# A two-block decoder kernel: the inverses of 32-token blocks built row by row, or row by row within 16 tokens and joined by products

## The chip, the cores and the metric

The kernel runs on one core of a Trainium2 chip. The metric is the device time of one execution in microseconds. The engines named below are TensorE (PE, with PEld for its weight loads), VectorE (DVE), ScalarE (ACT), GpSimd (POOL) and SyncE (SP), which only issues transfers here.

## The reference, cut to what matters

The reference is a decoder of several blocks over 16 meta tokens and 256 tokens of width 1024: feed-forward blocks, one RWKV-7 time mixing, sparse attention, and a second block with two kinds of attention. Only the time mixing is touched. Its core is a recurrence by token over a 64x64 state for each of 16 heads:

```python
def step(S, inp):
    r_t, w_t, k_t, v_t, a_t, b_t = inp
    sa = jnp.einsum("bhij,bhj->bhi", S, a_t)
    S = S * w_t[:, :, None, :] + sa[..., None] * b_t[:, :, None, :] + v_t[..., None] * k_t[:, :, None, :]
    y = jnp.einsum("bhij,bhj->bhi", S, r_t)
    return S, y
```

with `a = -kk` (the normalised removal keys) and `b = kk * a`. All is float32.

## The kernel before, in words

The kernel does not step token by token. It takes the 16 meta tokens as one chunk and the 256 others as four chunks of 64. Within a chunk the removals depend on each other through a strictly lower triangular matrix (the products of b with a), so each chunk and head needs the inverse of a unit lower triangular 64x64 matrix. `aab(m)` makes these products for the heads 2m and 2m+1, in blocks of 32 tokens: the 128 diagonal blocks (16 heads, 4 chunks, 2 blocks) go to `Dg`, those beside them to `Tt`. `inverses` inverts the diagonal blocks, and `doubles` makes the 64-token inverses of them by products (`da`, `db`).

`inverses` works with one block on each of the 128 partitions. `start` transposes `Dg` by 32x32 squares to `af` and sets `tf` to unit matrices. `rows` then runs over the rows s of a block: all rows below s get `a[:, s, i]` times row s added, as one multiplication into `u` (L868) and one addition (L871), each in two halves; for the last five rows one combined operation for every row below (L885). `end` transposes the result back twice, into `D1` (L891) and `Dt` (L892), and copies `Dt` into the diagonal blocks of `Tt`, half by ScalarE (L899), half by GpSimd (L901). `meta` does the same for the blocks of 16 of the meta chunk, on tiles named `am`.

The code is a list of steps in the order of the table `ORDER`: `solve0` to `solve8` are the steps that `inverses` returns, set among units of weights such as `v7` or `r0` (a unit: load 512 KB of weights, split them into two parts `wh` and `wl`, at L173 or L175 and L182, and multiply, at L261 to L263), the gates' low-rank products `g1a` and `g1b` (L614), evacuations such as `evr0`, and the steps of the recurrence (`ck`, `cv`, `cw`, `cr`, `cs`, `ct`, `cy`, `cn`). A scheduler of the framework then orders all instructions by a simulated timeline; each engine executes its own list strictly in that order. The tiles `mm` are PSUM banks (eight in rotation), `wl` has three buffers and `wh` four.

Names in the rows: `xmh`, `xml` are the two parts of the values' input, `xh`, `xl` those of the receptances'; `Tm` is the inverse of the meta chunk and `room` work space of the recurrence; `s`, `t` and `u` are temporary tiles.

Of the kernel before, what the change touches and what calls it, by code (L numbers as in the profile page):

```python
# [10 lines left out]
F32 = mybir.dt.float32  # L11
F32R = mybir.dt.float32r
I32 = mybir.dt.int32
AF = mybir.ActivationFunctionType
ALU = mybir.AluOpType
# [87 lines left out]
class Unit:  # L103
    """Weights to stream in, the products with them, and what follows some units later; held: units before that
    this one's products still read."""
# [6 lines left out]
class Core:  # L112
    def __init__(self, ctx, tc, io):
# [25 lines left out]
        self.eps = self.const.tile([128, 2], F32, name="eps")  # L139
# [8 lines left out]
    def call(self, fn, ahead=0):  # L148
        """fn between units; before it the parts of as many of those that follow, if they are not there yet."""
        self.items.append((fn, ahead))  # L150
# [16 lines left out]
    def hi(self, u):  # L167
        """Weights in two parts that single-pass products carry exactly: the first."""
        if not u.lo:
            return  # L170
        u.wh = self.wring.tile([128, 1024], F32R, tag="wh", name="wh", bufs=WH)[:u.p, :u.n]
        if u.hi == "A":
            self.A.activation(u.wh, u.wf[:u.p, :u.n], AF.Copy)  # L173
        else:
            self.V.tensor_copy(u.wh, u.wf[:u.p, :u.n])  # L175

    def lo(self, u):
        """And the second."""
# [5 lines left out]
    def run(self):  # L184
        units = [x for x in self.items if isinstance(x, Unit)]
        n = len(units)
# [3 lines left out]
        def ahead(i, most=WH):  # L190
            """Loads, first and second parts as far ahead of unit i as their rings reach."""
# [44 lines left out]
    def evac(self, name, out, x, scale=None):  # L236
        """Copies x, by ScalarE or VectorE."""
# [17 lines left out]
    def one(self, pool, name, shape, dt=F32):  # L255
        """A tile that keeps its place as long as the pool."""
# [12 lines left out]
    def accum(self, out, wh, wl, xh, xl, kn, n, k0=0, total=None):  # L269
        """out[m] += sum over k of w[k][m] x[k], weights standing, up to n columns of x moving."""  # L270
# [6 lines left out]
    def rsqrt(self, out, x, scale, eps):  # L277
        """1 / sqrt(x * scale + eps), with a Newton step."""
# [24 lines left out]
    def rms(self, n):  # L303
        """1 / rms by token, on every partition."""
# [5 lines left out]
    def split_tile(self, k, gain, t0, n):  # L310
        """Tile k of h * gain in two parts; its squares added up."""
# [11 lines left out]

    def swiglu(self, win, wout, t0, n, hook, first=()):
        """Reads the split of h that the step before left; hook(k) follows each finished tile of h."""
# [50 lines left out]
    def out_units(self, w, kn, src, scale, t0, n, hook, k0=0, eng=lambda m: {}):  # L376
        """h += scale * x @ w, x split and by features, w given as [m][128][kn][128]; a step a tile of h."""
# [28 lines left out]
    def play(self, order, steps, units):  # L406
        """Emits the steps by name: those of units as they come, the others as calls between them."""
# [7 lines left out]

    def rwkv(self, gain, hook):
# [21 lines left out]
        # the mixed inputs of the projections  # L438
# [6 lines left out]
        def mixes(i, kind, e=None):  # L445
            """Mixed input i, a tile a call: whole, or in two parts."""
# [35 lines left out]
        def first_mix():  # L482
            """The normalised input; the mixed inputs of the keys, the decays and the removals."""
            hn, xx, last = R["hn"], R["xx"], []
            hi, lo = R["x", 2] = [self.xs.tile([128, KT, T], F32R, tag=n, name=n) for n in ("xh", "xl")]
            def mix(x, i, k):
                """Mixed input i, by VectorE, or by ScalarE and GpSimdE."""
# [69 lines left out]
        # keys  # L557
# [18 lines left out]
        def first(n, parts):  # L576
            """The first tiles of the keys and the low-rank pairs of two inputs side by side, as the inputs come."""
# [23 lines left out]
        # low-rank pairs, in float32 products  # L601
        def l1_unit(c0, parts, k0, k1, last, after=()):
            """Columns c0.. of the first factors: parts are (bank, row, width, input)."""
# [67 lines left out]
        # a, b, k by decays within a chunk  # L671
# [5 lines left out]
        def units(q):  # L677
            """1 / norm of the keys."""
# [22 lines left out]
        def over(e, j, x, s):  # L701
            """KB[place j] = x / decay, for the pairs s; the factor -1/2 of place 0 comes with the products."""
# [19 lines left out]
        # strictly lower parts of b a by chunk: diagonal blocks of 32 tokens apart from those beside them  # L722
# [43 lines left out]
        # values, receptance, bonus  # L766
# [24 lines left out]
        # gates  # L791
# [63 lines left out]
    def inverses(self, R):  # L855
        """Inverses of unit lower triangular blocks of 32 tokens (16 in the meta chunk), one per partition."""
        V, G = self.V, self.G
# [18 lines left out]

        def rows(s0, s1):
            a, t = R["af"], R["tf"]
            for s in range(s0, s1):
                if s < B - 5:  # L880
                    u = self.tmp("u")[:, :(B - 1 - s) * (s + 1)].rearrange("p (a b) -> p a b", b=s + 1)
                    row(V, a, t, u, s + 1, s, (s + 1, (s + B + 1) // 2, B))
                else:
                    for i in range(s + 1, B):
                        V.scalar_tensor_tensor(t[:, i, :s + 1], t[:, s, :s + 1], a[:, s, i:i + 1], t[:, i, :s + 1],  # L885
                                               op0=ALU.mult, op1=ALU.add)

        def end():
            D1, Dt = R["D1"], R["Dt"] = R["Dg"], R["af"]
            tf, Tt = R["tf"], R["Tt"]  # L890
            V.transpose(D1, tf.rearrange("p s t -> p t s"))  # L891
            V.transpose(Dt, tf)  # L892
            Dt = Dt.rearrange("p t (m c) -> p m c t", c=NC)
# [26 lines left out]
        cuts = (0, 5, 10, 15, 20, 25, 31)  # L920
        return [start, meta] + [lambda a=a, b=b: rows(a, b) for a, b in zip(cuts[:-1], cuts[1:])] + [end]

    def chunks(self, R):
        """The recurrence over chunks of 64 tokens after the 16 of the meta tokens.
# [1121 lines left out]
```

## Time and profile before

| | |
|---|---|
| three runs | 1602.51, 1602.21, 1589.57 us; median 1602.21 |
| span of the profiled execution | 1588.7 us (30959 instructions), mean granted TensorE clock 0.971 |
| TensorE products busy | 1527.4 us (96%) |
| VectorE busy | 1020.3 us (64%) |
| ScalarE busy | 732.4 us (46%) |
| GpSimd busy | 334.0 us (21%) |

The profile is of one execution; its span is to be compared with the lowest of the three runs. A busy TensorE is one with a product in flight, not one at its peak. A float32 product leaves two records in the trace. The granted clock is 1.00 at 2.4 GHz and 0.50 at 1.2 GHz. Times in the views are counted from the start of the span.

### The profile page before, as it was taken

What the parts mean: (1) busy time and instruction counts of PE and PEld (TensorE: products, weight loads), DVE (VectorE), ACT (ScalarE), POOL (GpSimd) and SP (SyncE); (2) the same over time, 40 slices, a digit from 0 to 9 for tenths busy, and PEclk for the clock granted to TensorE, in tenths of its full rate; (3) what the DMA queues carried; (4) which work ended last, traced back from release to release, by engine and by line L of the source; (5) the groups of instructions that cost most, each with busy time, mean ns of one, the idle gap of its engine ahead of it and who ended that gap; (6) DMA issues with size and microseconds to landing.
All of it is one profiled execution on the core that took longest, in us unless ns stands there. A gap on an engine that the chain in (4) does not pass through costs nothing.

```text
span 1588.7 us, 30959 instructions
## 1 busy us (share of the span) xinstructions
PE 1527.4 (96%) x12612; PEld 1427.2 (90%) x12612; DVE 1020.3 (64%) x1857; ACT 732.4 (46%) x1266; POOL 334.0 (21%) x346
## 2 busy tenths in 40 slices
PE   7999989699999999999999999899999999999999
PEld 7999967568788999999999987579999978899999
DVE  6655478997444655556555569667665489886643
ACT  6544428333223544445444434655445335566532
POOL 2111034752011111001111043142110334320000
PEclk9999989798888999999999999999999999999999
DMA  7645534121101445555545552036556552265552
GB/s 224 216 173 166 178 96 141 63 92 69 41 1 41 173 173 175 171 175 191 175 174 165 172 166 77 21 112 234 186 183 180 175 167 91 85 215 186 187 195 101
DMA packets 70851, 230.63 MB, mean 145 GB/s; under 512 B 7827, under 2 KB 12468, under 8 KB 70580
## 3 DMA queue, kind: packets, MB, share of 16 engines
q1 hardware_dynamic: 68480, 225.35, 42.7%
q10 hardware_dynamic: 2228, 3.29, 0.9%
q8 instruction: 99, 1.62, 0.4%
q14 instruction: 44, 0.36, 0.1%
HBM read 226.52 MB, written 2.10 MB: 144 GB/s over the span
## 4 chain that ended last, share of the span: by engine, by line
PE 82%; DVE 12%; ACT 2%; DMA 2%; issue 1%; POOL 1%; SPq 0%; DVEq 0%; POOLq 0%; ACTq 0%
PE mm L261 22%; PE mm L262 22%; PE mm L263 22%; DVE wl L182 1%; PE mm L1064 1%; PE mm L1892 1%; PE mm L1063 1%; PE mm L1166 1%; PE mm L1165 1%; PE mm L1167 1%; DVE tf L871 1%; DMA wf<-ffn_in 1%; PE mm L994 1%; DVE u L868 1%; PE mm L1869 1%
## 5 line engine op out<-in xcount | busy, mean ns | idle before, releaser
L173 ACT ACTIVATE wh<-wf 128x1024 fp32r<-128x1024 f32 (+2 forms) x404 | 411.8, 1020 | 538.3 <-issue 284.3
L261 PE MATMUL mm<-xh,wh 128*128 128x272 f32 (+2 forms) x1888 | 544.4, 290 | 14.7 <-ACT wh L173 9.0
L182 DVE TENSOR_TENSOR wl<-wf,wh 128x1024 fp32r<-128x1024 f32 (+2 forms) x388 | 463.1, 1194 | 140.7 <-PE mm L263 96.5
L262 PE MATMUL mm<-xl,wh 128*128 128x272 f32 (+2 forms) x1888 | 542.0, 288 | 3.1 <-DVE xl L440 2.7
L263 PE MATMUL mm<-xh,wl 128*128 128x272 f32 (+2 forms) x1888 | 542.4, 288 | 1.7 <-DVE wl L182 1.7
L261 PEld LDWEIGHTS mm<-xh,wh 128*128 128x128 f32 (+1 forms) x1888 | 356.8, 190 | 21.9 <-ACT wh L173 9.9
L262 PEld LDWEIGHTS mm<-xl,wh 128*128 128x128 f32 (+1 forms) x1888 | 357.2, 189 | 7.5 <-DVE xl L440 3.8
L263 PEld LDWEIGHTS mm<-xh,wl 128*128 128x128 f32 (+1 forms) x1888 | 357.5, 190 | 3.2 <-DVE wl L182 2.7
L261 PE MATMUL mm<-hh,wh 128*128 128x272 f32 (+1 forms) x704 | 201.9, 287 | 0.0
L263 PE MATMUL mm<-hh,wl 128*128 128x272 f32 (+1 forms) x704 | 201.7, 287 | 0.0
L262 PE MATMUL mm<-hl,wh 128*128 128x272 f32 (+1 forms) x704 | 201.7, 287 | 0.0
L352 POOL TENSOR_TENSOR s<-s,rstd 128x272 f32<-128x272 f32 (+1 forms) x88 | 74.6, 849 | 442.8 <-ACT s L351 442.8
L182 POOL TENSOR_TENSOR wl<-wf,wh 128x1024 fp32r<-128x1024 f32 (+3 forms) x58 | 121.3, 2093 | 146.5 <-PE mm L263 63.5
L261 PEld LDWEIGHTS mm<-hh,wh 128*128 128x128 f32 x704 | 132.6, 188 | 0.0
L263 PEld LDWEIGHTS mm<-hh,wl 128*128 128x128 f32 x704 | 132.5, 188 | 0.0
L262 PEld LDWEIGHTS mm<-hl,wh 128*128 128x128 f32 x704 | 132.5, 188 | 0.0
L360 DVE TENSOR_TENSOR u<-mm,s 128x272 f32<-128x272 f32 (+1 forms) x88 | 38.5, 437 | 123.8 <-PE mm L263 108.2
L298 POOL TENSOR_TENSOR acc<-acc,sq 128x272 f32<-128x272 f32 (+1 forms) x48 | 41.4, 863 | 262.9 <-ACT sq L296 247.1
L350 DVE TENSOR_TENSOR t<-mm,rstd 128x272 f32<-128x272 f32 (+1 forms) x88 | 38.2, 436 | 69.8 <-PE mm L263 69.7
L261 PE MATMUL mm<-hid,wh 128*128 128x256 f32 x256 | 72.0, 281 | 0.0
L262 PE MATMUL mm<-hid,wh 128*128 128x256 f32 x256 | 72.0, 281 | 0.0
L263 PE MATMUL mm<-hid,wl 128*128 128x256 f32 x256 | 72.0, 281 | 0.0
(482 smaller groups left out, 2320.4 us busy)
## 6 DMA issues: line engine op xcount, KB each, us to landing
wf<-ffn_in SPq DMA_DIRECT2D x176, 512.0 KB, 3.6
wf<-ffn_out SPq DMA_DIRECT2D x64, 512.0 KB, 3.5
wf<-b_ff SPq DMA_DIRECT2D x64, 512.0 KB, 4.7
wf<-ffn_out SPq DMA_DIRECT2D x32, 384.0 KB, 3.1
wf<-rk_k SPq DMA_DIRECT2D x8, 512.0 KB, 3.4
wf<-rk_v SPq DMA_DIRECT2D x8, 512.0 KB, 3.8
wf<-rk_r SPq DMA_DIRECT2D x8, 512.0 KB, 3.2
wf<-rk_o SPq DMA_DIRECT2D x8, 512.0 KB, 3.2
```

The lines of the kernel that those rows point to most:

```text
L173: self.A.activation(u.wh, u.wf[:u.p, :u.n], AF.Copy)
L182: (self.V if u.lo == "V" else self.G).tensor_tensor(u.wl, u.wf[:u.p, :u.n], u.wh.bitcast(F32), op=ALU.subtract)
L261: self.mm(out, wh, xh, start=start, stop=False)
L262: self.mm(out, wh, xl, start=False, stop=False)
L263: self.mm(out, wl, xh, start=False, stop=stop)
L298: self.G.tensor_tensor(self.acc[:, :n], self.acc[:, :n], self.sq[:, :n], op=ALU.add)
L350: V.tensor_tensor(t[:, :n], st.pop(("g", m))[:, :n], r, op=ALU.mult)
L352: G.tensor_tensor(s[:, :n], s[:, :n], r, op=ALU.mult)
L360: V.tensor_tensor(u[:, :n], st.pop(("u", m))[:, :n], st.pop(("s", m))[:, :n], op=ALU.mult)
L868: e.tensor_tensor(tmp[:, x - o:y - o, :w], a[:, s, x:y, None].to_broadcast([P, y - x, w]), t[:, s:w, :w].to_broadcast([P, y - x, w]), op=A ...
L871: e.tensor_tensor(t[:, x:y, :w], t[:, x:y, :w], tmp[:, x - o:y - o, :w], op=ALU.add)
L994: mm(ps[h][:, j * w:(j + 1) * w], flat(src(c, m)[OWN[h]]), R["AR"][OWN[h], m, j0:j0 + n, tok(c)], start=True, stop=True)
```

## The change

Rows are done only within blocks of 16 tokens. Both halves of a 32-token block are handled by one operation (an access pattern with a step of 16 rows and 16 columns), so `rows` runs over 15 rows with one multiplication and one addition each. The part below, between the two halves, is then made by products on TensorE: `turned` transposes and multiplies the part of `Dg` below by the first inverse (L906), `joined` copies that to `tf`, clears the other half of `tf`, and multiplies by the second inverse, once for `Dt` in all four groups of 32 partitions (L916) and once in the other orientation for `Dg` in two groups (L918), and `added` adds the results (L924, L927). `end` keeps only the copies to `Tt`. A third column of `eps` holds a mask made of `tri` (L877). The number of steps stays nine, so `ORDER` is unchanged. The rest of the diff drops comments.

```diff
-        self.eps = self.const.tile([128, 2], F32, name="eps")
+        self.eps = self.const.tile([128, 3], F32, name="eps")
...
             begin(G, R["tf"], B)
 
+            G.tensor_scalar(self.eps[:, 2:3], self.tri[:, 0, n:n + 1], -1.0, 1.0, op0=ALU.mult, op1=ALU.add)
+
         def rows(s0, s1):
+
             a, t = R["af"], R["tf"]
+
+            def both(x, i, j, *dims):
+
+                at = x[:, i:i + 1, j:j + 1]
+                return bass.AP(tensor=at.tensor, offset=at.offset, ap=[at.ap[0], [n * B + n, 2]] + [list(d) for d in dims])
+
             for s in range(s0, s1):
-                if s < B - 5:
-                    u = self.tmp("u")[:, :(B - 1 - s) * (s + 1)].rearrange("p (a b) -> p a b", b=s + 1)
-                    row(V, a, t, u, s + 1, s, (s + 1, (s + B + 1) // 2, B))
-                else:
-                    for i in range(s + 1, B):
-                        V.scalar_tensor_tensor(t[:, i, :s + 1], t[:, s, :s + 1], a[:, s, i:i + 1], t[:, i, :s + 1],
-                                               op0=ALU.mult, op1=ALU.add)
+                m, w = n - 1 - s, s + 1
+                u = self.tmp("u")[:, :2 * m * w].rearrange("p (b i j) -> p b i j", b=2, j=w)
+                below = both(t, w, 0, (B, m), (1, w))
+                V.tensor_tensor(u, both(a, s, w, (1, m), (0, w)), both(t, s, 0, (0, m), (1, w)), op=ALU.mult)
+                V.tensor_tensor(below, below, u, op=ALU.add)
+
+        quads = [slice(32 * q, 32 * q + 32) for q in range(4)]
+        byblk = lambda p: p.rearrange("p (c j) -> p c j", j=n)
+
+        def turned():
+
+            tf, Dg, Dt = R["tf"], R["Dg"], R["af"]
+            V.transpose(Dg[:, :n], tf[:, :, :n].rearrange("p s t -> p t s"))
+            V.transpose(Dt, tf)
+            p = R["p16"] = self.psum()
+            for c in range(32):
+                for r in quads:
+                    mm(p[r, c * n:c * n + n], Dg[r, :, c], Dg[r, :n, c], start=True, stop=True)
+
+        def joined():
+            tf, Dg, Dt = R["tf"], R["Dg"], R["af"]
+            V.transpose(Dg[:, n:], tf[:, :, n:].rearrange("p s t -> p t s"))
+            self.A.activation(tf[:, :, :n], byblk(R.pop("p16")), AF.Copy)
+            G.memset(tf[:, :, n:], 0.0)
+            p, o = R["p16"] = self.psum(), self.psum()
+            for c in range(32):
+                for r in quads:
+                    mm(p[r, c * n:c * n + n], tf[r, c], Dt[r, n:, c], start=True, stop=True)
+                for r in quads[::2]:
+                    mm(o[r, c * n:c * n + n], Dt[r, :, c], tf[r, c, :n], start=True, stop=True)
+
+        def added():
+            Dg, Dt = R["Dg"], R["af"]
+            p, o = R.pop("p16")
+            x = Dt[:, n:].rearrange("p t c -> p c t")
+            V.tensor_tensor(x, byblk(p), x, op=ALU.add)
+            for r in quads[::2]:
+                x = Dg[r, :n].rearrange("p t c -> p c t")
+                V.scalar_tensor_tensor(x, byblk(o)[r], self.eps[r, 2:3], x, op0=ALU.mult, op1=ALU.add)
 
         def end():
-            D1, Dt = R["D1"], R["Dt"] = R["Dg"], R["af"]
-            tf, Tt = R["tf"], R["Tt"]
-            V.transpose(D1, tf.rearrange("p s t -> p t s"))
-            V.transpose(Dt, tf)
-            Dt = Dt.rearrange("p t (m c) -> p m c t", c=NC)
+            R["D1"], R["Dt"] = R["Dg"], R["af"]
+            Tt = R["Tt"]
+            Dt = R["Dt"].rearrange("p t (m c) -> p m c t", c=NC)
...
-        cuts = (0, 5, 10, 15, 20, 25, 31)
-        return [start, meta] + [lambda a=a, b=b: rows(a, b) for a, b in zip(cuts[:-1], cuts[1:])] + [end]
+        cuts = (0, 5, 10, 15)
+        return [start, meta] + [lambda a=a, b=b: rows(a, b) for a, b in zip(cuts[:-1], cuts[1:])] + [turned, joined, added, end]
```

The lists of the engines change as follows. TensorE, at the end of the gates' low-rank products (L614), before:

```order
L614 MATMUL mm<-xm,wf 32x272
L614 MATMUL mm<-xm,wf 64x272 x2
L614 MATMUL mm<-xm,wf 32x272
L261 MATMUL mm<-xmh,wh 128x272
L262 MATMUL mm<-xml,wh 128x272
```

The unit v7 (L261 and L262 with `xmh` and `xml`) came directly behind them. And now:

```order
L614 MATMUL mm<-xm,wf 32x272
L906 MATMUL mm<-tf 32x16 x128
L916 MATMUL mm<-af,tf 32x16 x4
L918 MATMUL mm<-tf,af 32x16 x2
L916 MATMUL mm<-af,tf 32x16 x4
L918 MATMUL mm<-tf,af 32x16 x2
```

All 320 new products (the four and two of L916 and L918 come 32 times) stand ahead of v7, r0 and the recurrence's first products, which keep their order among themselves.

VectorE, from the eighth row of the meta chunk (`am`) on, before:

```order
L868 TENSOR_TENSOR am<-am 128x8x8
L868 TENSOR_TENSOR u<-af,tf 128x84
L868 TENSOR_TENSOR u<-af,tf 128x91
L871 TENSOR_TENSOR am<-am 128x8x8
L871 TENSOR_TENSOR tf<-tf,u 128x12x7
L871 TENSOR_TENSOR tf<-tf,u 128x13x7
```

and now, from a row later:

```order
L892 TENSOR_TENSOR u<-af,tf 128x128
L871 TENSOR_TENSOR am<-am 128x7x9
L893 TENSOR_TENSOR tf<-tf,u 128x2x8x8
L868 TENSOR_TENSOR am<-am 128x6x10
L892 TENSOR_TENSOR u<-af,tf 128x126
L871 TENSOR_TENSOR am<-am 128x6x10
```

Each operation on the blocks is now one in place of two, and the rows of the blocks end with those of the meta chunk in place of 16 rows later.

GpSimd, behind the clearing of the keys' tile `KBt`, before:

```order
L963 MEMSET KBt 128x1024
L182 TENSOR_TENSOR wl<-wf,wh 128x1024
L1003 MEMSET room 128x512
L182 TENSOR_TENSOR wl<-wf,wh 128x1024 x2
L977 MEMSET UV 64x1024
L182 TENSOR_TENSOR wl<-wf,wh 128x1024 x2
L901 COPY Tt<-af 32x16x32 x4
```

and now:

```order
L957 COPY Tm<-s 128x8x8
L1002 MEMSET KBt 128x1024
L912 MEMSET tf 128x32x16
L940 COPY Tt<-af 32x16x32 x4
L1042 MEMSET room 128x512
L182 TENSOR_TENSOR wl<-wf,wh 128x1024 x3
```

The four copies to `Tt` (L901 before, L940 now) stood behind five second parts `wl` of weights and now stand ahead of them, as ScalarE's four copies (L899, now L938) do ahead of the first part of r3's weights.

## Rows read from the trace of the kernel before

**Rows 1.** The page's chain that ended last: shares of the span by engine.
```profile
PE 82%; DVE 12%; ACT 2%; DMA 2%; issue 1%; POOL 1%; SPq 0%; DVEq 0%; POOLq 0%; ACTq 0%
```

**Rows 2.** The chain from 300 to 400 us: shares by line.
```profile
by line: DVE tf L871 15.3%; DVE u L868 12.1%; PE mm L261 6.7%; PE mm L262 6.1%; PE mm L263 5.8%; POOL s L916 4.1%; DVE kbx L706 4.0%; DVE AR L717 3.5%; PE mm L1126 3.3%; PE mm L1037 2.6%; ACT Tt L899 2.4%; DVE tf L743 2.3%; PE mm L994 2.1%;
```

**Rows 3.** TensorE by stretch: length, busy us (records), granted clock, DMA share, GB/s.
```profile
314.67:320.00 5.33, 5.33 (x25) 0.54 0.02 5
332.55:371.84 39.29, 32.35 (x325) 0.87 0.20 68
344.00:348.00 4.00, 4.00 (x28) 0.64 0.29 116
360.00:368.00 8.00, 7.24 (x53) 0.57 0.20 68
378.00:382.00 4.00, 4.00 (x22) 0.62 0.40 131
```

**Rows 4.** Timeline of TensorE: start, us, instruction, [idle before <-releaser].
```profile
343.68 0.60 PE L262 MATMUL mm<-xl,wh 128*128 128x272 f32 x1 [2.74 <-DVE xl L440]
360.76 2.60 PE L1037 MATMUL mm<-room,Tm 16*16 16x64 f32 x32 [3.65 <-DVE room L241]
```

**Rows 5.** VectorE's groups by line from 319 to 367 us: busy, mean ns.
```profile
L871 DVE TENSOR_TENSOR tf<-tf,u 128x110 f32<-128x110 f32 (+32 forms) x54 | 19.7, 399 | 0.1
L868 DVE TENSOR_TENSOR u<-af,tf 128x110 f32<-128x110 f32 (+32 forms) x54 | 15.7, 329 | 0.0
```

**Rows 6.** Timeline of VectorE in the rows of the inverses.
```profile
319.62 0.18 DVE L868 TENSOR_TENSOR am<-am 128x15 f32<-128x15 f32 x1
320.06 0.19 DVE L868 TENSOR_TENSOR am<-am 128x28 f32<-128x28 f32 x1
320.17 2.48 DVE L868 TENSOR_TENSOR u<-af,tf 128x15 f32<-128x15 f32 x2
322.67 0.26 DVE L871 TENSOR_TENSOR tf<-tf,u 128x15 f32<-128x15 f32 x2
339.62 0.48 DVE L868 TENSOR_TENSOR u<-af,tf 128x128 f32<-128x128 f32 x2
340.03 2.65 DVE L871 TENSOR_TENSOR tf<-tf,u 128x128 f32<-128x128 f32 x2
366.46 2.04 DVE L891 STREAM_TRANSPOSE tf<-tf 128x1024 f32<-128x1024 f32 x1
```

**Rows 7.** Timeline of GpSimd in the same stretch.
```profile
320.22 2.39 POOL L182 TENSOR_TENSOR wl<-wf,wh 128x1024 fp32r<-128x1024 f32 x1 [4.67 <-PE mm L263]
337.20 1.10 POOL L916 COPY s<-am 128x128 f32<-128x128 f32 x1 [4.62 <-DVE am L871]
371.47 4.88 POOL L901 COPY Tt<-af 32x512 f32<-32x512 f32 x4
```

**Rows 8.** Timeline of TensorE: small products, each with what starts behind it.
```profile
306.78 0.35 PE L738 MATMUL mm<-AR,kbx 64*32 64x32 f32 x7
306.99 0.35 PE L738 MATMUL mm<-AR,kbx 64*32 64x32 f32 x7
...
348.11 0.69 PE L1008 MATMUL mm<-AR,kbx 64*16 64x16 f32 x64
348.73 0.39 PE L261 MATMUL mm<-xh,wh 128*128 128x272 f32 x1
...
372.45 1.07 PE L1118 MATMUL mm<-tf,Tt 32*32 32x32 f32 x32
373.46 0.69 PE L1048 MATMUL mm<-UV,KBt 128*64 128x64 f32 x16
```

**Rows 9.** Timeline of ScalarE: an eviction of a whole PSUM bank.
```profile
458.55 0.60 ACT L239 ACTIVATE room<-mm 128x512 f32<-128x512 f32 x1 [0.55 <-PE mm L1020]
```

**Rows 10.** The tile `tri`: time to landing; and GpSimd's timeline at the start.
```profile
DMA to landing us min/median/max: 7.1/7.1/7.1
9.59 1.70 POOL L298 TENSOR_TENSOR acc<-acc,sq 128x272 f32<-128x272 f32 x2 [3.08 <-ACT sq L296]
```

More of the change, by code (lines that the diff above doesn't have):

```diff
@@ L855, in inverses @@
     def inverses(self, R):
-        V, G = self.V, self.G
+        V, G, mm = self.V, self.G, self.mm
         NC, B, n = SEQ // 64, 32, NMETA
```

## The prediction

> **What bounds the kernel now.** I read the page's shares first, then the chain that ended last, then the stretch it points to. Over the whole span TensorE carries 82% of the chain and VectorE 12% [rows 1], so a saving on VectorE counts only where the chain runs through VectorE. The chain from 300 to 400 us shows that stretch: the two lines of the row-by-row inverses, L871 and L868, are its largest shares, 15.3% and 12.1% of 100 us, and the copies of the finished inverses on ScalarE (L899) stand in it too [rows 2]. What the chain does not say is how much TensorE would do there if VectorE were never late. From the end of the gates' low-rank products (332.55) to the first product with the keys by token (371.84) there are 39.29 us, of which TensorE is busy 32.35 [rows 3]. The 6.9 us of idle are almost all in two waits for VectorE, 2.74 and 3.65 [rows 4]. Part of the busy time is slow time: the granted clock is 0.64 on the mean from 344 to 348 and 0.57 from 360 to 368, so part of it at 1.2 GHz; at full clock the work of these two windows, 4.00 and 7.24 us, would take 1.4 and 3.1 less [rows 3]. So TensorE has 32.35 - 4.5 = 27.8 us of work in these 39.3, and **11.5 us is the most that any relief of VectorE can win here**. The 35 us that VectorE is busy with L868 and L871 for the blocks [rows 5] would be the wrong figure to take.
>
> **The change, part by part.**
>
> Removed from VectorE: 108 operations of L868 and L871 and the ten of L885. Not all of their time is work: a pair on 15 and 16 elements took 2.48 us while GpSimd ran a `wl` of 2.39 from the same moment; the next such pair took 0.26 [rows 6, 7]. GpSimd's `wl` stay, so stalls of 2.2 us stay too.
>
> Added on VectorE, the rows: 30 operations, interleaved with 30 of the meta chunk as before. Three small ones that depend on each other start 0.44 us apart, first to third (319.62 to 320.06); a pair of 128 elements takes 0.41 from start to start (339.62 to 340.03) [rows 6]. A step is now two operations of the meta chunk and two of the blocks, so 0.44 at the ends and some 0.66 in the middle; I take 0.57, and 15 steps give 8.6 us from 319.6. To that come a stall behind the `wl` at 320.22 (2.2), a second behind the next `wl` (2.2), and the meta chunk's two small transposes, which now stand among the rows together with the copies that they wait for, 1.10 us each by the undisturbed row [rows 7]: some 2.3. Rows done: 319.6 + 8.6 + 2.2 + 2.2 + 2.3 = 334.9, where L891 followed them at 366.46 before.
>
> Added on VectorE, the rest: a transpose of half the blocks, half of the 2.04 us of L891 [rows 6], ends at 335.9. The full transpose, four small operations for r0 and the gates, and the second half transpose follow by some 340. After the products come L924 and two L927. They end long before anything needs them.
>
> Moved on TensorE: 320 small products now stand between the low-rank products and v7 (L906, 128 of them; then L916 and L918, 192), and TensorE takes its instructions in order. That gives four terms.
> - Wait for the first half transpose: 335.9 - 332.55 = **3.3 us**. Queued behind it are v7, r0 and everything of the recurrence. Without the second stall and the waits for the copies it would be nothing; with them longer, 4.
> - L906, 256 records (a float32 product leaves two). No row has 32 x 32 tiles in four places with 16 columns. The nearest below is L1008, 16 weights and 16 columns over four tiles: 64 records, then the next product 0.62 us after the first, 9.7 ns each. The nearest above is L1118, 32 weights and 32 columns over two tiles, one operand strided as here: 32 records in 1.01 us, 31.6 ns. Between them lies L738 with L741, 32 weights over four tiles: 12 records from 306.78 to 306.99, 17.5 ns, at the half clock that stood there [rows 8]. I take the last, whose weights and tiles are most alike: **4.5 us** (2.5 to 8.1).
> - Wait until those are copied and the other half is cleared: ScalarE's copy of 128x512 takes 0.60 [rows 9], with the handing over **0.8 us** (0.3 to 1.5). The clearing on GpSimd, behind the second half transpose at some 340, lies beside L906 and this copy.
> - L916 and L918, 384 records at the same price: **6.7 us** (3.7 to 12.1).
>
> What the products do to the clock: behind the small products that end at 314, full-width products ran from 314.67 to 320 at a mean of 0.54, so 2.5 of 5.33 us were lost [rows 3]. I add **2.5 us** (1 to 3) for v7 and what follows it.
>
> Two queues get a wait that they did not have. ScalarE's and GpSimd's copies to `Tt` now stand ahead of the weights' parts of r3 and r2, and wait for L924 at some 348. GpSimd's four take 4.88 us [rows 7], a `wl` behind them 2.39, so r2's is there at about 356; TensorE reaches r2 at some 365, after v7, r0, the meta chunk's products and r1. I cost this at nothing: about 9 us of cover, and some 3 us if it were gone. The one column added to `eps`, early on GpSimd, waits for `tri`, which lands 7.1 us after its issue, between two sums for which GpSimd waits 3.08 us on ScalarE anyway [rows 10]: nothing.
>
> After 371.84 the `Tt` copies are no longer near the chain. Before, they lay ahead of a slow stretch, 0.62 of the clock from 378 to 382, 1.5 us lost [rows 3]. I take half of it, **-0.8 us** (0 to -1.5).
>
> Sum: 3.3 + 4.5 + 0.8 + 6.7 + 27.8 + 2.5 = 45.6 us in place of 39.3, so +6.3, and with the last term **+5.5 us**. The profiled span of 1588.7 becomes 1594. That execution belongs with the fastest of the three runs shown (1589.57); the other two are at 1602, so executions of one kernel differ by 0.8%. Put on the median: 1602.2 + 5.5 = 1608.
>
> A rule weighed here. The records of L1008 follow each other by 9.7 ns [rows 8]. The Trainium skill (TensorE: Matmul & The Clock Gate, section "Wait — 56ns, not 53.3ns?") says that matmuls never start closer than about 25 ns, however few their columns. By that 640 records are an estimated 16 us, and the time would be some 1613. The trace disagrees where successive products use different tiles, and the sum goes by its rows.
>
> **The rivals.**
> - *Slower: the new products overlap as little as L1118 does.* For it: 32 weights and a strided operand as there, and L918 uses only two of the four tiles. Against it: four tiles and half the columns. 640 records at 31.6 ns are 20.2 us in place of 11.2, so +14.5: 1617. A loss it is in any case; it passes 1% from some 34 ns a record on. The Trainium skill's rule above would lead this way.
> - *Faster: they run like L1008, and the transposes come in time.* 0 + 2.5 + 0.3 + 3.7 + 27.8 + 1.0 = 35.3, so -4.0, with all of the last term -5.5: 1597. For it: four tiles and 16 columns. Against it: VectorE's two new waits for copies.
> - *It takes its 30 us from VectorE, and nothing moves.* New products and waits just fill the 11.5 us that TensorE had spare: 1602, between the two others.
> - *The queues behind the `Tt` copies decide.* If L924 came past 357, r2 would wait for its `wl`, some 3 us: 1611. Against it: 9 us of cover.
>
> **How the numbers follow.** Forecast, TensorE pays some 5 us: 0.5. Like L1008: 0.2. Nothing moves: 0.1. Like L1118: 0.15. Queues: 0.05. The likeliest gives 1608, and the cases by themselves span 1597 to 1617. The spread of executions adds its own bound: were the median to fall on the fast side, each case would lie some 12 us lower, 1585 to 1605, which I hold for one time in three. Leaving out a tenth at either end gives 1588 to 1616. A measurement of this kernel can tell about 1% (16 us) from no change. Slower by more: the upper half of the L1118 case, 0.08. Faster by more: the L1008 case met by a fast median, 0.05. Within 1%: 0.87.
>
> **What would show it.** On VectorE: 15 operations each of L892 and L893, the last before 337. On TensorE: idle of 0 to 4 us ahead of L906 and about 1 ahead of L916; records of L906 10 to 32 ns apart, which decides among the cases; L918 ending between 340 and 356; no wait of more than 1 us ahead of r1, r2 or the products with `Tm`; the clock at 0.50 in part of v7; and the first L1087 near 378. A TensorE wait of more than 5 us anywhere from 332 to 400, or more than 3 us won or lost outside that stretch, would make this wrong.

## The result, and the profile after

Over 16 executions of each, the kernel before takes 1597.93 us (median) and the changed one 1604.03. The ratio on record, which is not that of the two medians (they lie 6.1 us apart), is 1.0055 with an interval of [1.0034, 1.0076], so the change costs 8.8 us (5.4 to 12.1). The profiled execution spans 1599.5 us against 1588.7.

The page of the changed kernel: busy times of the engines, and of its DMA queues the one that brings instructions (packets, MB, share). The same queue of the kernel before follows in a fence of its own.

```profile
PE 1533.4 (96%) x13252; PEld 1434.4 (90%) x13252; DVE 1000.0 (63%) x1773; ACT 733.0 (46%) x1267; POOL 330.6 (21%) x348
q8 instruction: 104, 1.70, 0.4%
```

```profile
q8 instruction: 99, 1.62, 0.4%
```

VectorE is 20 us less busy, TensorE 6 us more. The queue carries five packets of 16 KB more; they turn out to matter.

The stretch of the prediction, from the end of the gates' low-rank products to the first product with the keys by token, in the changed kernel. Columns as in [rows 3]: length, busy us (records), granted clock, DMA share, GB/s. The first row is the whole, the next four are L906, the wait behind it, L916 with L918, and the rest; the last is the recurrence.

```profile
333.94:382.14 48.20, 39.77 (x966) 0.79 0.18 57
336.70:341.93 5.23, 4.09 (x256) 0.59 0.04 12
341.93:343.71 1.78, 0.01 (x2) 0.50 0.00 0
343.71:353.89 10.18, 7.42 (x384) 0.50 0.02 5
353.89:382.14 28.25, 28.25 (x328) 0.93 0.24 76
382.14:518.91 136.77, 134.06 (x1565) 0.86 0.09 29
```

The stretch takes 48.2 us where [rows 3] had 39.29. TensorE's timeline says where the 8.9 us more are (start, us, instruction, idle before and its releaser; of the rows of L916 and L918 only those behind an idle time stand here):

```profile
336.70 2.38 PE L906 MATMUL mm<-tf 32*32 32x16 f32 x151 [2.77 <-DVE tf L901]
340.21 1.72 PE L906 MATMUL mm<-tf 32*32 32x16 f32 x105 [1.14 <-issue]
343.71 0.30 PE L916 MATMUL mm<-af,tf 32*32 32x16 f32 x8 [1.77 <-POOL tf L912]
...
347.85 0.18 PE L916 MATMUL mm<-af,tf 32*32 32x16 f32 x1 [1.29 <-issue]
...
351.85 0.24 PE L916 MATMUL mm<-af,tf 32*32 32x16 f32 x3 [1.47 <-issue]
```

Two idle times have a releaser: 2.77 us for the half transpose L901, and 1.77 for the clearing L912. Three have none ("issue"): 1.14, 1.29 and 1.47 us, 3.9 us that the prediction did not have.

VectorE and GpSimd at the same places:

```profile
321.63 2.39 DVE L892 TENSOR_TENSOR u<-af,tf 128x30 f32<-128x30 f32 x1
...
327.37 2.46 DVE L892 TENSOR_TENSOR u<-af,tf 128x126 f32<-128x126 f32 x1
...
335.55 1.00 DVE L901 STREAM_TRANSPOSE tf<-tf 128x512 f32<-128x512 f32 x1
...
341.97 1.04 DVE L910 STREAM_TRANSPOSE tf<-tf 128x512 f32<-128x512 f32 x1 [2.31 <-PE mm L906]
```

```profile
321.55 2.42 POOL L182 TENSOR_TENSOR wl<-wf,wh 128x1024 fp32r<-128x1024 f32 x1 [4.52 <-PE mm L263]
327.33 2.35 POOL L182 TENSOR_TENSOR wl<-wf,wh 128x1024 fp32r<-128x1024 f32 x1
...
343.13 0.52 POOL L912 MEMSET tf<- 128x512 f32 x1 [3.96 <-DVE tf L910]
```

The rows end at 335.3 with the two foreseen stalls beside GpSimd's `wl`. The second half transpose (L910) waits for TensorE: it overwrites the half of `Dg` that L906 reads as weights.

### The profile page after: what moved, and what is told of

It is laid out like the page before. It is cut to its first block, busy times and chain, and to the rows that moved or that the text cites. A ratio compares the mean times of both kernels' runs of the same rounds, so it can differ in the third digit from the quotient of the medians.

```text
span 1599.5 us, 32160 instructions
## 1 busy us (share of the span) xinstructions
PE 1533.4 (96%) x13252; PEld 1434.4 (90%) x13252; DVE 1000.0 (63%) x1773; ACT 733.0 (46%) x1267; POOL 330.6 (21%) x348
## 4 chain that ended last, share of the span: by engine, by line
PE 83%; DVE 10%; ACT 2%; DMA 2%; issue 1%; POOL 1%; SPq 0%; DVEq 0%; POOLq 0%; ACTq 0%
PE mm L261 22%; PE mm L262 22%; PE mm L263 22%; PE mm L1931 1%; DVE wl L182 1%; PE mm L1103 1%; PE mm L1205 1%; PE mm L1204 1%; PE mm L1206 1%; PE mm L1102 1%; DMA wf<-ffn_in 1%; PE mm L1033 1%; PE mm L1908 1%; PE mm L1933 1%; PE mm L1875 1%
## 5 line engine op out<-in xcount | busy, mean ns | idle before, releaser
L261 PE MATMUL mm<-xh,wh 128*128 128x272 f32 (+2 forms) x1888 | 542.9, 289 | 13.8 <-ACT wh L173 8.7
L262 PE MATMUL mm<-xl,wh 128*128 128x272 f32 (+2 forms) x1888 | 540.3, 287 | 0.0
L261 PEld LDWEIGHTS mm<-xh,wh 128*128 128x128 f32 (+1 forms) x1888 | 355.5, 189 | 20.7 <-ACT wh L173 9.5
L262 PEld LDWEIGHTS mm<-xl,wh 128*128 128x128 f32 (+1 forms) x1888 | 355.7, 189 | 3.8 <-issue 2.1
L261 PE MATMUL mm<-hh,wh 128*128 128x272 f32 (+1 forms) x704 | 201.9, 287 | 0.0
L262 PE MATMUL mm<-hl,wh 128*128 128x272 f32 (+1 forms) x704 | 201.7, 287 | 0.0
L261 PEld LDWEIGHTS mm<-hh,wh 128*128 128x128 f32 x704 | 132.6, 188 | 0.0
L262 PEld LDWEIGHTS mm<-hl,wh 128*128 128x128 f32 x704 | 132.5, 188 | 0.0
L261 PE MATMUL mm<-hid,wh 128*128 128x256 f32 x256 | 72.0, 281 | 0.0
L262 PE MATMUL mm<-hid,wh 128*128 128x256 f32 x256 | 72.0, 281 | 0.0
```

The costliest lines, as they stand in the source:

```text
L261: self.mm(out, wh, xh, start=start, stop=False)
L262: self.mm(out, wh, xl, start=False, stop=False)
```

## The experiments

### What relief of VectorE is worth: no products

```diff
-            for c in range(32):
-                for r in quads:
-                    mm(p[r, c * n:c * n + n], Dg[r, :, c], Dg[r, :n, c], start=True, stop=True)
...
-                    mm(p[r, c * n:c * n + n], tf[r, c], Dt[r, n:, c], start=True, stop=True)
...
-                    mm(o[r, c * n:c * n + n], Dt[r, :, c], tf[r, c, :n], start=True, stop=True)
```

> This kernel keeps the rows within 16 tokens, the transposes, the copies and the sums, but leaves out all 320 products between the halves (so its result is not the reference's; the copies read other data in their place). It prices the relief of VectorE alone. My theory, that the changed kernel gained what VectorE gave back and lost more than that to the products on TensorE: the stretch from the end of the gates' low-rank products to the first product with the keys by token falls from 39.3 us (before) and 48.2 (changed) to 28 to 31, and the time to 8 to 11 us under before. Rival: TensorE's waits in the stretch were not VectorE's doing and others take their place: stretch 35 to 39 us, time less than 4 us under before.

> As the run without products, and without the three sums (L924, L927) too, which had moved ahead of the mix of r0's input on VectorE and there cost 6 us (again not the reference's result). What VectorE's relief is worth when nothing stands in its place. If TensorE's own work sets the floor (27.8 us at full clock): stretch 28.5 to 31.5 us against 39.3 before, full-clock equivalent of the span (span times mean granted clock) 7 to 10 us under before's 1543. Rival: what follows, the chain of the meta chunk through VectorE, ScalarE and TensorE, cannot go faster than it does, and the stretch stays above 34.

Measured: without products 0.9969 [0.9947, 0.9991], 4.9 us under before; without the sums too 0.9958 [0.9935, 0.9982], 6.7 us (2.9 to 10.4). My theory's stretch came out in neither: the first (36.45 us) has its rival's, the second (33.46 us) lies between the two. TensorE's waits from 325 to 375 us (total, times, longest) and the stretch, first without products, then without the sums too:

```profile
PE mm L262 <- DVE xl L440: 6.5, 1, 6.5
332.59:369.04 36.45, 29.57 (x325) 0.86 0.25 81
```

```profile
PE mm L261 <- ACT xh L466: 3.3, 1, 3.3
331.42:364.88 33.46, 30.21 (x325) 0.90 0.26 87
```

Without products and sums the stretch is 33.5 us, not 28, and the wait that remains is for the last mix of r0's input (L466 on ScalarE, from what L461 makes on VectorE). VectorE and ScalarE of that run:

```profile
336.73 0.59 DVE L461 SCALAR_TENSOR_TENSOR t<-hn,hv,s 128x272 f32<-128x272 f32 x1
```

```profile
336.94 4.36 ACT L923 ACTIVATE Tt<-af 32x512 f32<-32x512 f32 x4
341.32 0.43 ACT L466 ACTIVATE xh<-t 128x272 fp32r<-128x272 f32 x1
```

The mix could have run at 337.3. It stood in ScalarE's queue behind the four copies to `Tt`, which in the changed kernel come behind it and here, with no product or sum left to wait for, ahead of it. In the first run its second part (L440) stood behind the sums in VectorE's queue in the same way. Each of the two kernels thus has a wait of its own making, and neither measures the bound of 11.5 us. What they show is that VectorE's relief gave 6.7 us in the better of them; the changed kernel is some 15 us above that.

### Where the products stand

```diff
-         "solve5 evv1 g1b solve6 solve7 evv5 solve8 v7 evv6 r0 evv7 ck0 evr0 dropv cv0 cm0 r1 evrb0 co0 r2 "
+         "evv1 g1b evv5 v7 solve5 evv6 r0 solve6 evv7 ck0 evr0 dropv cv0 cm0 r1 solve7 solve8 evrb0 co0 r2 "
```

> The changed kernel with one line of the order moved: the first products (L906) stand behind v7, the second (L916, L918) behind r0. Theory 1, TensorE is held up by the supply of its instructions, in pieces of 128 records some 3.8 us apart: v7 covers the wait for the rows (2.8 us), r0 the wait between the two groups (1.8), and one to two of the three pauses stay (1.2 to 1.5 each), since 256 and 384 records still follow each other without cover: stretch 42 to 44 us, time 2 to 5 us over before. Theory 2, the pauses belong to the place (to what VectorE or a transfer does at 339, 346 and 350 us): the pauses stay three, or vanish, whatever stands ahead.

Measured: 1.0048 [1.0028, 1.0068], 7.7 us over before where 2 to 5 were expected; the stretch is 45.41 us, above the expected 42 to 44. TensorE with L906 behind v7, the pauses of the second group, and the windows of L906 and r0:

```profile
335.97 3.85 PE L906 MATMUL mm<-tf 32*32 32x16 f32 x255
341.02 0.24 PE L906 MATMUL mm<-tf 32*32 32x16 f32 x1 [1.21 <-issue]
...
351.39 0.24 PE L916 MATMUL mm<-af,tf 32*32 32x16 f32 x3 [0.87 <-issue]
...
355.39 0.18 PE L918 MATMUL mm<-tf,af 32*32 32x16 f32 x1 [1.56 <-issue]
...
335.97:339.82 3.85, 3.84 (x256) 1.00 0.03 11
341.19:346.94 5.75, 5.75 (x32) 0.52 0.28 94
```

Both waits with a releaser are gone. Three pauses stay, 3.6 us, where theory 1 had one or two; by their number this is theory 2, and in time two of them overlap the old ones. What decides is their place in the program. Counted from the start of the execution, they stand behind 2777, 3032 and 3160 of TensorE's records; in the changed kernel they stand behind 2649, 2904 and 3032, in `own` (below) behind 2649, 2776, 2904 and 3032. These are steps of 128 to within one record: the pauses go with the instructions, not with the time. The last row is r0 (and 8 records of L916), run at 0.52 of the clock behind L906: 24 products, which as v7 in this run took 3.2 us at full clock, took 5.7. One unit ahead of each group takes away both waits (4.5 us); the stretch keeps 2.8 us of it, and the time 1.1, which the intervals do not tell from nothing.

### What the pauses are

`own`, `twice` and `relief` were executed once each; only their profiles are read. `own`, a transpose that need not wait for L906:

```diff
-            V.transpose(Dg[:, n:], tf[:, :, n:].rearrange("p s t -> p t s"))
+            Dx = R["Dx"] = self.wide_pair("s")
+            for i in range(2):
+                V.transpose(Dx[i], tf[:, :, n + 8 * i:n + 8 * i + 8].rearrange("p s t -> p t s"))
...
+            for i, x in enumerate(R.pop("Dx")):
+                V.tensor_copy(Dg[:, n + 8 * i:n + 8 * i + 8], x)
```

> The changed kernel with the second half transpose (L910) into temporaries, so that it need not wait until the first products have read the tile; two small copies put it in place after the last products. Waits simply add up: TensorE's wait between the two groups falls from 1.78 to some 0.7 us and the stretch with it, 1.05 us less. Supply of instructions in pieces of 128 records: the wait falls in the same way, but 23 records into the second group a pause of about 1 us appears that was not there before, and the stretch stays within 0.3 us of 48.2.

`twice`, each product of L906 two times:

```diff
-                for r in quads:
+                for r in quads + quads:
                     mm(p[r, c * n:c * n + n], Dg[r, :, c], Dg[r, :n, c], start=True, stop=True)
```

> The changed kernel with each of the 128 first products (L906) issued twice, 256 records more. Supply of instructions in pieces of 128 records, 3.8 us each: two pauses more, and the stretch grows by 7.2 to 8 us. The engine's own pace is all that counts: 256 records at 16 ns, 4.1 us, and no further pause.

TensorE of `own`, rows behind an idle time (its second group is L918 and L920):

```profile
336.52 2.37 PE L906 MATMUL mm<-tf 32*32 32x16 f32 x151 [3.25 <-DVE tf L901]
340.54 1.72 PE L906 MATMUL mm<-tf 32*32 32x16 f32 x105 [1.65 <-issue]
343.04 0.30 PE L918 MATMUL mm<-af,tf 32*32 32x16 f32 x8 [0.78 <-ACT tf L913]
...
344.45 0.18 PE L920 MATMUL mm<-tf,af 32*32 32x16 f32 x1 [0.84 <-issue]
```

The wait is 1.0 us shorter, and a pause of 0.84 us stands where none was, 22 records into the group. The stretch is 48.19 us, as long as in the changed kernel (48.20), although L901 came 0.5 later.

TensorE of `twice`, L906 alone:

```profile
336.78 2.36 PE L906 MATMUL mm<-tf 32*32 32x16 f32 x151 [2.80 <-DVE tf L901]
340.57 2.02 PE L906 MATMUL mm<-tf 32*32 32x16 f32 x128 [1.44 <-issue]
344.30 2.02 PE L906 MATMUL mm<-tf 32*32 32x16 f32 x128 [1.71 <-issue]
348.03 1.71 PE L906 MATMUL mm<-tf 32*32 32x16 f32 x105 [1.70 <-issue]
```

Between pauses exactly 128 records, 3.73 us from start to start, of which 2.02 run. There are five pauses in all for three, as expected. The stretch is 55.02 us, 6.8 more for 256 records: a little under the 7.2 to 8 of the supply, far from the 4.1 of the pace.

That 128 records are one packet of the instruction queue follows from counts of that queue in all profiles: 99 packets before and without products, 101 with 256 small records, 103 with 512, 104 with 640, 106 with 896. In the changed kernel two packets can be seen, the only traffic of the 5 us from 340 (GB/s in 40 slices of 0.125 us):

```profile
GB/s 0 0 0 0 0 0 0 0 0 0 131 0 0 0 0 0 0 0 0 0 0 0 0 0 0 0 0 0 0 0 0 0 0 0 0 0 0 0 0 131
DMA packets 2, 0.03 MB, mean 7 GB/s; under 512 B 0, under 2 KB 0, under 8 KB 0
```

The first begins at 341.3, 1.1 us after TensorE had gone on at 340.21, the second at 345.0, 2.9 us before it goes on at 347.85; each takes 1.3 us. The reading that fits all runs: a packet is asked for when the one before it is begun, and its instructions can be issued 3.0 to 4 us later; an engine that uses up 128 records sooner waits. In `mix` (below) 128 records take 4.3 to 5.8 us, and there is no pause. That the request comes at that moment is inferred from the spacing, not shown.

### The stalls beside GpSimd

```diff
-       "lov": "GVGGVVGV", "lor": "GGGGGGGG", ...
+       "lov": "GVGGVVVV", "lor": "VGGGGGGG", ...
```

> The changed kernel with the second parts of v6's and r0's weights made by VectorE in place of GpSimd. If a VectorE operation stands for some 2.2 us whenever GpSimd runs such a part beside it: the operations of 2.4 us among the rows (there are two) become at most one, and the rows end 1 to 3 us earlier, so TensorE's wait ahead of L906 falls from 2.8 us to 0.3 to 1.8. Rival: VectorE loses as much by making the parts (1.2 us each) and the wait stays 2.4 to 3.2.

```profile
338.84 2.36 PE L906 MATMUL mm<-tf 32*32 32x16 f32 x151 [0.30 <-DVE tf L901]
344.46 1.72 PE L906 MATMUL mm<-tf 32*32 32x16 f32 x105 [3.27 <-issue]
```

One long operation is left among the rows (2.45 us), and the wait for L901 falls from 2.77 to 0.30, as the theory of the stalls has it. But the first pause grows from 1.14 to 3.27 us, and the stretch is still 47.25. In this run 512 KB of r's weights were landing from 339.3 to 342, and the instruction packet began only at their end, at 342.1; in the changed kernel the load had ended near 337, and the packet began at 337.8. That the load held the packet up is likely and was not tried apart. Of the 2.5 us gained on VectorE 2.1 came back as a longer pause.

### Fewer products, and products mixed in

`turn` drops L918 and lets VectorE transpose the finished inverses:

```diff
-                for r in quads[::2]:
-                    mm(o[r, c * n:c * n + n], Dt[r, :, c], tf[r, c, :n], start=True, stop=True)
...
-            for r in quads[::2]:
-                x = Dg[r, :n].rearrange("p t c -> p c t")
-                V.scalar_tensor_tensor(x, byblk(o)[r], self.eps[r, 2:3], x, op0=ALU.mult, op1=ALU.add)
+            V.transpose(Dg.rearrange("p s c -> p c s"), Dt.rearrange("p t c -> p c t"))
```

> The changed kernel without the 64 products in the other orientation (L918): VectorE transposes the finished inverses instead, one operation of some 1.2 to 2 us where it has nothing else to do. Supply of instructions in pieces of 128 records: a whole piece less, so its 2.5 us and its pause of 1.3 to 1.5 go, stretch 48.2 - 3.9 = 44.3 us (43.6 to 45), time 4 to 6 us over before. Pace alone: 128 records at 19.5 ns, stretch 45.7. The transposition on the path: stretch 46 or more.

`mix` adds to it that `accum` issues some small products behind each step of a unit (`R["fill"]` is a list of such groups, eight for the first products and sixteen for the second; `solve7` and `solve8` stand behind `evrb2` now):

```diff
             self.mm3(out, wh[:, s], wl[:, s], xh[:, k0 + k, :n], xl[:, k0 + k, :n], k0 + k == 0, k0 + k == total - 1)
+            if fill:
+                fill.pop(0)()
...
-         "solve5 evv1 g1b solve6 solve7 evv5 solve8 v7 evv6 r0 evv7 ck0 evr0 dropv cv0 cm0 r1 evrb0 co0 r2 "
+         "evv1 g1b evv5 v7 solve5 evv6 r0 solve6 evv7 ck0 evr0 dropv cv0 cm0 r1 evrb0 co0 r2 "
```

> As the kernel with the transposition, and the small products mixed with the large ones: behind each three products of r0 sixteen of L906, behind each three of r1 and of r2 eight of the second group. Supply of instructions: 128 records now hold 11 to 20 large products and take 3.3 to 4.2 us, so pauses fall to under 1.1 us in all; with the waits covered by v7 and r0 TensorE has 27.8 + 8.2 us of work, and with 1 to 2.5 us of half clock the stretch is 37 to 39.5 us: level with before, time 3 us under to 1 us over it. Rival: going from products on the whole array to products on a quarter of it and back costs each time, 24 times 0.1 to 0.2 us, stretch 40 to 44, time 1 to 5 us over before.

`turn`: 1.0017 [0.9994, 1.0040], the loss of the changed kernel down to 2.7 us (-1.0 to 6.4). The stretch is 42.05 us, 2.3 better than expected. The second group, now 256 records on four tiles:

```profile
348.02 2.22 PE L916 MATMUL mm<-af,tf 32*32 32x16 f32 x150 [1.77 <-POOL tf L912]
351.34 1.62 PE L916 MATMUL mm<-af,tf 32*32 32x16 f32 x106 [1.10 <-issue]
```

256 records in 3.84 us are 15.0 ns each, where L916 and L918 together took 7.42 us for 384, 19.3 ns. The group with L918, a third of it on two tiles only, is the slower one per record; whether L918's records alone lose the time or the others beside them too is not shown.

`mix`: 1.0001 [0.9979, 1.0024], level with before and 8.6 us under the changed kernel. The stretch, and one period of r0 with its sixteen small products (32 records; L910 is this kernel's number for L906):

```profile
332.16:371.04 38.88, 38.88 (x839) 1.00 0.23 77
...
338.04 0.65 PE L910 MATMUL mm<-tf 32*32 32x16 f32 x32
338.62 0.39 PE L261 MATMUL mm<-xh,wh 128*128 128x272 f32 x1
338.85 0.29 PE L262 MATMUL mm<-xl,wh 128*128 128x272 f32 x1
338.97 0.28 PE L263 MATMUL mm<-xh,wl 128*128 128x272 f32 x1
339.19 0.65 PE L910 MATMUL mm<-tf 32*32 32x16 f32 x32
```

TensorE is busy for all of 38.88 us at a granted clock of 1.00: no wait, no pause, nothing at 1.2 GHz. But the period is 1.15 us. Three large products are 0.38 of it (each starts 0.125 behind the last), so 32 records cost 0.77, or 24 ns each where they run at 15 to 16 by themselves; the change of tile size costs an estimated 0.14 us each way (half of 0.77 less the 0.50 of 32 records alone). The Trainium skill (TensorEngine Tiling (Array Packing), section "Key Properties") says that changing the tiling drains TensorE; the rows agree in that each change costs time, and do not show what is done in it. Stretch and time are those expected of the supply, although the rival's price of 0.1 to 0.2 us a change came too: the 1 to 2.5 us of half clock that were expected did not. Mixing does not make the products cheap; it saves the waits, the pauses and the clock.

### One group of products

`half` subtracts the first 16 rows also from the 16 below (L893, L897, up to 256 elements an operation), so that the first group is not needed, mixes the second into r1 and r2, and keeps the transposition of `turn`:

```diff
+                w, m = s + 1, n - 1 - s
+                top, low = B - 1 - s, n + s
...
+                V.tensor_tensor(u, a[:, s, w:, None].to_broadcast([128, top, w]), t[:, s:w, :w].to_broadcast([128, top, w]), op=ALU.mult)
...
+                V.tensor_tensor(t[:, w:, :w], t[:, w:, :w], u, op=ALU.add)
```

> A version of the idea with one group of products in place of two: the rows of the first 16 tokens are also subtracted from the 16 below (32 operations more on VectorE, some 5 us), so that only the multiplication by the second inverse is left to TensorE, 128 products or 256 records, eight behind each three products of r1 and r2. If TensorE's work sets the stretch, as the mixed kernel's 38.9 us without a wait suggest: 38.9 - 4.1 = 34.8 us and what r0's last mix is late behind the longer rows, 1 to 3 us, so 36 to 38 us; time 1 to 5 us under before. Rival: the longer rows on VectorE come back as waits of 3 to 6 us with half clock behind them, stretch 38 to 41, time level with before or up to 4 us over it.

`halft` takes temporaries from other rings:

```diff
-                z = self.tmp("t")[:, :m * w].rearrange("p (a b) -> p a b", b=w) if m else None
+                z = self.tmp("u")[:, :m * w].rearrange("p (a b) -> p a b", b=w) if m else None
...
-            w, x = self.wide_pair("s"), self.wide_pair("s")
+            w, x = self.wide_pair("s"), self.wide_pair("t")
```

> As the run before, with two temporaries of the meta chunk taken from another ring, so that the last mix of r0's input does not wait for the meta chunk's last copy. If that mix is what TensorE waits for behind r0: its wait is 1 to 2 us shorter than in the run before, and the time 1 to 3 us under that one's; otherwise the same.

`half`: 0.9982 [0.9957, 1.0007], 2.9 us under before, with an interval that reaches over 1. `halft`: 0.9962 [0.9943, 0.9981], 6.1 us under before (3.0 to 9.1): the one version with the whole computation that beats both kernels beyond its interval. The stretches, `half` first:

```profile
333.35:372.30 38.95, 35.45 (x582) 0.91 0.23 70
```

```profile
334.82:372.70 37.88, 34.62 (x581) 0.95 0.23 72
```

The wait for r0's last mix is 3.5 and 3.3 us, so the rival's wait did come, with its stretch of 38 to 41 in `half`, and the other ring did not shorten it by the expected 1 to 2 us. The two kernels' intervals overlap; that the ring makes the difference is not shown.

### The kernel before once more

> The kernel before once more, unchanged, for a second profile and for the clocks of its single executions. If the spread of some 12 us between executions of one kernel comes from TensorE's granted clock, span times mean clock is the same for all of them within 2 us (1541 to 1545), and the stretch from the end of the low-rank products is 39.3 us within 0.5. Rival: it comes from late transfers at the start, and the spans differ at one clock.

Against the other executions of the same kernel it measures 1.0013 [0.9988, 1.0038]. Its second profile; the stretch, then the recurrence. Behind it the recurrence in the profile of [rows 3]:

```profile
333.21:369.19 35.98, 30.82 (x325) 0.91 0.24 74
369.19:515.78 146.59, 142.47 (x1566) 0.79 0.08 27
```

```profile
371.84:508.05 136.21, 134.02 (x1566) 0.86 0.08 29
```

The expectation of 39.3 within 0.5 fails: the stretch is 3.3 us shorter here, and the recurrence 10.4 us longer, at 0.79 of the clock in place of 0.86. At full clock the recurrence would take 115.8 us here and 117.1 there (length times clock). Most of the spread of spans is the clock's: over the 79 executions of before they go from 1587 to 1602 us, the longer ones at the lower clock, while span times mean clock stays within 1540 and 1550 (the clock is given to three digits, 0.8 us either way). So that product is less constant than the 2 us expected, and the rival is not wholly out: at one clock, 0.971, the spans still go from 1588.7 to 1595.1. The clock is the larger part; where the rest comes from was not looked into, nor why an execution gets the lower clock (the longer recurrence also has 4.1 us of idle TensorE for 2.2).

| | executions | mean span | mean clock | span x clock |
|---|---|---|---|---|
| before (three sets) | 21, 35, 23 | 1593.0, 1594.2, 1596.2 | 0.9695, 0.9688, 0.9682 | 1544.4, 1544.4, 1545.4 |
| changed | 16 | 1603.1 | 0.9658 | 1548.3 |
| `none3` | 12 | 1586.4 | 0.9712 | 1540.7 |
| `turn` | 12 | 1597.8 | 0.9680 | 1546.6 |
| `mix` | 12 | 1594.1 | 0.9716 | 1548.8 |
| `halft` | 12 | 1590.0 | 0.9730 | 1547.0 |

The changed kernel has 4 us more of full-clock time, and some 5 us more lost at 1.2 GHz (span less that product). `mix` has the same 4 us more and gives them back by a better clock; what `halft` wins is clock as well. `none3` has 3.7 us less of full-clock time than before, where 7 to 10 were expected. Of the executions of before that stand beside the changed kernel's in the result no clocks are on record, so these comparisons go across sets.

## Why the prediction was right, and where it was not

Its sign and its mechanism held: TensorE pays, VectorE's 20 us come to little. 1608 against 1604 and +5.5 against +8.8 us (5.4 to 12.1) are inside the range and within 1%, partly by luck. The loss was 3 us larger, and the median of 16 executions of the kernel before lies 4 us under that of the three shown. Within the sum two errors met: up to v7 the new waits and products took 20.0 us for 15.3, and what follows took 28.25 for 30.3.

- *The wait ahead of L906*: 2.77 for 3.3. The 15 operations of each kind, the last ending at 335.27, and the two stalls beside the `wl` came as said. The other parts did not: of the 2.3 us for the meta chunk's transposes some 0.4 came (L956 at 330.09, no wait for its copy), and the 15 steps took some 9.5 us for 8.6. L614 and the rows' start both came 1.4 us later than before.
- *L906*: 5.23 us for 4.5. The pace was 16.0 ns a record (4.09 us for 256) for 17.5: between the bounds. What was missing is the pause of 1.14.
- *The wait ahead of L916*: 1.78 for 0.8. The failing step is "the second half transpose follow by some 340": L910 writes what L906 reads. `own` shows that this alone cost next to nothing, because the next instructions were not there either.
- *L916 and L918*: 10.18 us for 6.7, inside 3.7 to 12.1. Running 7.42 (19.3 ns, L918's two tiles, named as a rival's point), pauses 2.76.
- *The rest with its clock*: 28.25 for 27.8 + 2.5. v7 ran at 0.50 for most of its time, as said, and took 5.0 us (353.89 to 358.89); before it took 3.1 (332.55 to 335.65). 28.25 us at 0.93 of the clock are 26.3 at the full one: the 27.8 was some 1.5 too high.
- *The sum*: 48.2 for 45.6 (the 39.3 of before is one profile's; in its second profile the stretch is 35.98). The term left out is the supply of instructions, 3.9 us. The trace of before had a row for it, in the products of `aab`, outside the stretch that I read; it is a pause without a releaser in a run of small products:

```profile
291.41 0.19 PE L741 MATMUL mm<-AR,kbx 64*32 64x32 f32 x1 [1.62 <-issue]
```

- *The Trainium skill's rule* (TensorE: Matmul & The Clock Gate, "Wait — 56ns, not 53.3ns?"), starts no closer than 25 ns, does not hold here: 15.0 to 16.4 ns over four tiles. Its time came close by the pauses: 24 ns a record all in all (15.4 us for 640).
- *The queues behind the `Tt` copies*: these started at 355.1 in place of 348 and delayed nothing: TensorE waits for no weights up to 400. Of the 9 us of cover 8 were left: r2's part was done at 362.9, and TensorE began r2 at 370.9.
- *The tail of -0.8* cannot be told: one stage of one kernel differs by 10 us between executions. For the same reason my bound of 3 us outside the stretch was no test: the clock alone can break it in a single profile.
- *The bound of 11.5 us* for any relief of VectorE was not reached and not refuted: the best kernel without products won 6.7, with a wait of 3.3 us left that its own order made.

## What to carry to other kernels

In this kernel a long run of small products cost three things that their own pace does not show: pauses for instructions (3.9 us), the clock during and behind the run, and the waits of an engine that takes its list in order. Mix them a few at a time between large products, and count the records: having fewer of them (`turn`, 6.1 us under the changed kernel) was worth more here than moving them (`later`, 1.1). Where executions differ, compare span times granted clock beside the span, and take a second profile of the kernel before before pricing a stretch to 1 us.

## What had not been expected of the hardware

- TensorE's instructions arrive during the run in packets of 16 KB, 128 records of products each. In the long runs the next 128 began 3.0 to 4.0 us after the last (3.73 twice in `twice`), 29 ns a record at 3.73, and beside a weight load 5.3 us (`relief`, from the 24th record of L906 at 339.2 to 344.46).
- Small products on four tiles run at 15.0 to 16.4 ns a record, at a granted clock of 0.50 (`turn`: 256 in 3.84 us) as at 1.00 (`later`: 255 of L906 in 3.85 us).
- Between executions of one kernel the granted clock differs, and most of the time with it: 0.79 and 0.86 over the same recurrence, 10 us.
